# Turned softmax weights split one unit later, and head 10 turned on TensorE

## The chip, the cores and the metric

The kernel runs on one core of one Trainium2 chip. The metric is the device time of one execution in microseconds (us); several runs are made and their median is taken. Five engines have instruction queues of their own, each worked through in order: TensorE (PE, with its weight loads PEld), VectorE (DVE), ScalarE (ACT), GpSimd (POOL) and SyncE (SP), which here issues most of the DMA transfers.

## What is computed

One layer of an encoder on 256 tokens of width 2048: a normed input projection, windowed attention of 12 query heads on 4 key/value heads beside a small Fourier mixing group, an output projection, and a gated feed-forward network with a short convolution. The change touches the attention alone. Of the reference, that part is:

```python
scores = jnp.einsum('bnqkgd,bnskd->bnkgqs', qb, kb).astype(jnp.float32)
scores = scores * (HEAD_DIM ** -0.5)
scores = scores + alibi[None, None]
scores = jnp.where(valid[None, :, None, None], scores, NEG_INF)
m = jnp.maximum(jnp.max(scores, axis=-1, keepdims=True), sink_b)
p = jnp.exp(scores - m)
p = p / (jnp.sum(p, axis=-1, keepdims=True) + jnp.exp(sink_b - m))
out = jnp.einsum('bnkgqs,bnskd->bnqkgd', p.astype(v.dtype), vb)
```

Everything is float32. Products are made from two parts of each operand, a rounded high part ("hi") and the rest ("lo"), in three matmuls: hi by hi, lo by hi, hi by lo. So each tile that goes into a product is first split: ScalarE writes the high part, VectorE subtracts it from the original and writes the low part.

## The kernel before

The weights come in tiles of 1 MB, and each tile is one *unit*. `unit(i, work)` issues, in this order: the work hung up under `before[i]` (small matmuls of the attention), the unit's own matmuls, the work under `beside[i]` (vector and scalar work of the attention), the split of the weight tile of unit i+2 (`split`, L181 on ScalarE and L182 on VectorE) with the load of tile i+5, and the work under `behind[i]`. There is no scheduler: this order is the order in each engine's queue. Units 4 to 7 project v; units 8 to 23 project the heads in the order k0 q0 q1 q2 k1 q3 q4 q5 k2 q6 q7 q8 k3 q9 q10 q11; units 24 to 39 are the output projection (`moving_weights`, L333 to L335), which from unit 24 on reads the finished heads from the tiles `cat`; after that comes the feed-forward part.

A query head that is projected in unit s passes through the following steps, each hung up some units later:

- s+1, beside: `qk_out` adds the two halves of the projection (L631 ScalarE, L633 VectorE), and `qk_parts` splits the result into `qT` (L269 ScalarE, L270 VectorE). A key head does the same with one more multiply (L635) into `kT` (L643, L644).
- s+2, before: `scores` (L654, six matmuls of qT and kT). Beside: `scores_out` (L670 to L675, VectorE). Behind: `exps` (L684, L688, ScalarE).
- s+3, beside: `weigh` normalises the weights (L693 to L697, VectorE).
- The weights must then be turned (transposed). For the heads in `FLIPS` (0 to 10) VectorE turns 32x32 blocks (`flip_out`, L314, also at s+3), four DMAs write them to HBM (L317), and at s+4 `flip_in` reads them back in turned order (one DMA, L325) into the tile `flop`. At s+5, beside, `flip_parts` splits `flop` into `pt` (L739 ScalarE, L740 VectorE, two instructions each). Head 11 is turned on TensorE instead: `turn` at s+4, before (L704, four transposes), `turn_out` at s+4, beside, splits the result (L716, L717).
- `values`, before (L749, six matmuls of pt and v), at s+6 for the heads in `FLIPS` and at s+5 for the other; `values_out` in the same unit, beside: `feature_out` splits the scaled result into `cat` (L269, L270), squares it (`sq`, L489, ScalarE) and sums the squares on GpSimd (L490).

Within one unit's beside work the order before the change is: weigh and flip_out, flip_in, qk_out, values_out, turn_out, flip_parts, qk_parts, scores_out. On TensorE it is: values, turn, scores, then the unit's own matmuls.

Since the slots 8, 12, 16 and 20 are key heads, which have no scores and no values, the steps of a unit repeat with a period of four. Below, "unit 22 on VectorE" means the beside work and the split that are issued with unit 22, whenever VectorE comes to them.

Of the kernel before, what the change touches and what calls it, by code (L numbers as in the profile page):

```python
# [18 lines left out]
NH = 12  # L19
# [33 lines left out]
for _g in range(NKV):  # L53
    QK_ORDER += [("k", _g)] + [("q", _g * GQA + _i) for _i in range(GQA)]

FLIPS = range(NH - 1)
QK_FIRST = {n: (2, 2) if n in (8, 12) else (1, 0) for n in range(16)}
N_U, N_V, N_QK = 0, 4, 8
N_OUT = N_QK + len(QK_ORDER)
# [45 lines left out]
def block_kernel(  # L105
# [111 lines left out]
    def u_part(k, o, n, m=1):  # L217

        rows = ux[k // 4][:, (k < 4) * U_HEAD :].rearrange("p (k c) -> p k c", k=4)
        return rows[:, k % 4 : k % 4 + m, o : o + n]  # L220
# [152 lines left out]
    before, beside, behind = {}, {}, {}  # L373

    def at(when, i, f, *a):
        when.setdefault(i, []).append((f, a))
# [17 lines left out]
    for k in range(NK):  # L394
# [3 lines left out]
        n = 1 if c < 2 else 2  # L398
# [3 lines left out]
        if q % n == 0:  # L402
            w, h = u_part(k, 0, FW, n), hi[:, q : q + n, :]
# [225 lines left out]
    def qk_out(kind, h, ps):  # L629
        tmp = ph.tile([P, S], F32, tag="tmp", name=f"tmp_{kind}{h}", bufs=2)  # L630
        nc.scalar.activation(tmp, ps[:, S : 2 * S], AF.Copy)  # L631
        add = ph.tile([P, S], F32, tag="add", name=f"add_{kind}{h}", bufs=2)
        nc.vector.tensor_tensor(add, ps[:, 0:S], tmp, ALU.add)  # L633
        if kind == "k":
            nc.vector.tensor_tensor(add, add, r1b, ALU.mult)  # L635
        st["add", kind, h] = add
# [125 lines left out]
    for i in range(N_QK, N_OUT + 8):  # L762
        heads = {i - s: h for (kind, h), s in slot_of.items() if kind == "q"}
        new = [kh for kh, s in slot_of.items() if i - s == 1]
        for n, h in sorted(heads.items()):
            if n == 5 + (h in FLIPS):
                at(before, i, values, h)
        if 4 in heads and heads[4] not in FLIPS:
            at(before, i, turn, heads[4])
        if 2 in heads:  # L770
            at(before, i, scores, heads[2])
        if 3 in heads:
            at(beside, i, weigh, heads[3])
            if heads[3] in FLIPS:
                at(beside, i, flip_out, heads[3])
        if 4 in heads and heads[4] in FLIPS:
            at(beside, i, flip_in, heads[4])
        for kind, h in new:
            at(beside, i, lambda k=kind, h=h: qk_out(k, h, st.pop(("ps", k, h))))
        for n, h in sorted(heads.items()):  # L780
            if n == 5 + (h in FLIPS):
                at(beside, i, values_out, h)
        if 4 in heads and heads[4] not in FLIPS:
            at(beside, i, turn_out, heads[4])
        if 5 in heads and heads[5] in FLIPS:
            at(beside, i, flip_parts, heads[5])
        for kind, h in new:
            at(beside, i, qk_parts, kind, h)
        if 2 in heads:
            at(beside, i, scores_out, heads[2])  # L790
            at(behind, i, exps, heads[2])
# [59 lines left out]
    for n, (c, kq) in enumerate(OUT_ORDER):  # L851
        i = N_OUT + n
# [397 lines left out]
    i = up_index[n]  # L1250
# [158 lines left out]
```

## Time and profile before

| what | value |
|---|---|
| median of three runs | 945.75 us (945.72 to 945.88) |
| profiled execution, its own time | 945.7 us |
| profiled execution, first to last instruction (span) | 943.9 us |
| mean granted TensorE clock | 0.998 of full speed |
| TensorE busy | 930.4 us, 99% of the span |
| VectorE busy | 768.0 us, 81% |
| ScalarE busy | 541.6 us, 57% |
| GpSimd busy | 50.9 us, 5% |
| flip to HBM (L317) | 44 DMAs of 64 KB, 3.3 us to landing |
| HBM back to flop (L325) | 11 DMAs of 256 KB, 4.1 us to landing |

The profile is of one execution. A row of the timeline reads: start and duration in us, engine, line of the kernel, operation, output and inputs by their names in the program, shape, count, and in brackets how long the engine had been idle before and what it waited for. Rows of one engine can overlap a little, since the next instruction starts before the last has drained. Views that sum up waits give the total in us, the number of waits and the longest one.

### The profile page before, as it was taken

How to read it: one execution, taken by the hardware profiler on the slowest of the kernel's cores; microseconds unless marked ns; L12 is line 12 of the kernel's file. 1: busy time of each engine (PE TensorE's matmuls, PEld its weight loads, DVE VectorE, ACT ScalarE, POOL GpSimd, SP SyncE). 2: the span in 40 equal slices, each digit the busy share in tenths (PEclk: the TensorE clock that was granted, in tenths of full speed). 3: DMA queues.
4: the chain of work that ended last, by engine and by line, in shares of the span. 5: the costliest groups of instructions: out<-in, count | busy, mean ns of one | idle time of the engine just before them, and what ended most of it. 6: DMA issues, size and time to landing. Idle time of an engine off the chain costs nothing.

```text
span 943.9 us, 12848 instructions
## 1 busy us (share of the span) xinstructions
PE 930.4 (99%) x5025; PEld 804.7 (85%) x5025; DVE 768.0 (81%) x968; ACT 541.6 (57%) x673; POOL 50.9 (5%) x68
## 2 busy tenths in 40 slices
PE   9999999999999999999999999999999999999996
PEld 7888888888888888888888888888888888888885
DVE  7658888776677778799787997878989779989886
ACT  7755666654454555566555565555655556655553
POOL 0100000000000000000000000000000000000002
PEclk9999999999999999999999999999999999999999
DMA  9965666645556578877897779877788978779652
GB/s 365 308 224 167 212 213 193 220 178 205 196 214 211 182 230 254 260 257 234 257 262 254 243 235 277 250 263 228 262 242 238 299 246 261 230 231 274 208 178 89
DMA packets 48588, 220.63 MB, mean 234 GB/s; under 512 B 15856, under 2 KB 19184, under 8 KB 24976
## 3 DMA queue, kind: packets, MB, share of 16 engines
q1 hardware_dynamic: 43984, 190.32, 55.8%
q0 software_dynamic: 4544, 29.49, 16.8%
q8 instruction: 39, 0.64, 0.3%
q14 instruction: 21, 0.17, 0.0%
HBM read 214.81 MB, written 4.98 MB: 233 GB/s over the span
## 4 chain that ended last, share of the span: by engine, by line
PE 80%; DVE 7%; DMA 5%; ACT 4%; issue 2%; SPq 1%; POOL 0%; DVEq 0%; POOLq 0%; ACTq 0%
PE ps_val L350 25%; PE ps_gate L350 25%; PE ps_P L1118 3%; PE ps_P L1119 3%; PE ps_P L1120 3%; DVE lo L182 3%; PE ps_N L1118 3%; PE ps_N L1119 3%; PE ps_N L1120 3%; ACT hi L181 3%; PE ps_a L335 2%; PE ps_a L333 2%; PE ps_a L334 2%; DMA chan<-in_c_chan 2%; DMA ux<-in_w_u_x 1%
## 5 line engine op out<-in xcount | busy, mean ns | idle before, releaser
L182 DVE TENSOR_TENSOR lo<-raw,hi 128x2048 fp32r<-128x2048 f32 (+1 forms) x129 | 293.4, 2274 | 45.1 <-ACT hi L181 44.8
L181 ACT ACTIVATE hi<-raw 128x2048 fp32r<-128x2048 f32 (+1 forms) x129 | 245.2, 1902 | 35.6 <-PE ps_a L334 13.3
L350 PE MATMUL ps_val<-hU,hi 128*128 128x512 f32 x688 | 236.2, 389 | 0.0
L350 PE MATMUL ps_gate<-hU,hi 128*128 128x512 f32 x688 | 236.2, 389 | 0.0
L350 PE MATMUL ps_val<-hU,lo 128*128 128x256 f32 x688 | 189.9, 276 | 0.0
L350 PE MATMUL ps_gate<-hU,lo 128*128 128x256 f32 x688 | 189.9, 276 | 0.0
L350 PEld LDWEIGHTS ps_val<-hU,hi 128*128 128x128 f32 x688 | 129.1, 188 | 26.8
L350 PEld LDWEIGHTS ps_gate<-hU,hi 128*128 128x128 f32 x688 | 129.1, 188 | 26.8
L350 PEld LDWEIGHTS ps_gate<-hU,lo 128*128 128x128 f32 x688 | 129.1, 188 | 1.3
L350 PEld LDWEIGHTS ps_val<-hU,lo 128*128 128x128 f32 x688 | 129.1, 188 | 1.3
L893 ACT ACTIVATE ft_g<-ps_gate 128x256 f32<-128x256 f32 x43 | 16.5, 384 | 123.0 <-PE ps_gate L350 123.0
L893 ACT ACTIVATE ft_v<-ps_val 128x256 f32<-128x256 f32 x43 | 16.5, 384 | 91.8 <-PE ps_val L350 91.8
L350 PE MATMUL ps_q<-hT,hi 128*128 128x512 f32 x192 | 65.0, 391 | 0.0
L1118 PE MATMUL ps_P<-hi_P,op_P 128*128 128x512 f32 x144 | 56.0, 389 | 0.0
L1119 PE MATMUL ps_P<-hi_P,op_P 128*128 128x512 f32 x144 | 56.0, 389 | 0.0
L1120 PE MATMUL ps_P<-lo_P,op_P 128*128 128x512 f32 x144 | 56.0, 389 | 0.0
L350 PE MATMUL ps_q<-hT,lo 128*128 128x256 f32 x192 | 51.1, 277 | 0.0
L1010 DVE TENSOR_TENSOR lo_N<-sumw,hi_N 128x2048 fp32r<-128x2048 f32 (+1 forms) x20 | 41.5, 2076 | 9.4 <-ACT hi_N L1009 9.2
L1118 PE MATMUL ps_N<-hi_N,op_N 128*128 128x512 f32 x108 | 42.0, 389 | 0.0
L1119 PE MATMUL ps_N<-hi_N,op_N 128*128 128x512 f32 x108 | 42.0, 389 | 0.0
L1120 PE MATMUL ps_N<-lo_N,op_N 128*128 128x512 f32 x108 | 42.0, 389 | 0.0
L350 PEld LDWEIGHTS ps_q<-hT,hi 128*128 128x128 f32 x192 | 35.2, 188 | 6.6
(386 smaller groups left out, 1584.8 us busy)
## 6 DMA issues: line engine op xcount, KB each, us to landing
raw<-in_w_up SPq DMA_DIRECT2D x86, 1024.0 KB, 5.6
raw<-in_w_in SPq DMA_DIRECT2D x20, 1024.0 KB, 5.4
raw<-in_w_out SPq DMA_DIRECT2D x16, 1024.0 KB, 4.8
sumw<-in_w_down POOLq DMA_DIRECT2D x16, 1024.0 KB, 8.6
raw<-in_w_down_late SPq DMA_DIRECT2D x4, 1024.0 KB, 7.2
raw<-in_w_down_last SPq DMA_DIRECT2D x4, 768.0 KB, 4.2
turnp<-flip SPq DMA_DIRECT2D x44, 64.0 KB, 3.3
flop<-turnp SPq DMA_DIRECT2D x11, 256.0 KB, 4.1
```

The source lines that it names most:

```text
L181: nc.scalar.activation(hi[:, 0:n], raw[:, 0:n], AF.Copy)
L182: nc.vector.tensor_tensor(lo[:, 0:n], raw[:, 0:n], f32(hi[:, 0:n]), ALU.subtract)
L333: nc.tensor.matmul(ps, ah, wh, start=first and q == q0, stop=False)
L334: nc.tensor.matmul(ps, al, wh, start=False, stop=False)
L335: nc.tensor.matmul(ps, ah, wl, start=False, stop=last and q == q0 + len(kk) - 1)
L350: nc.tensor.matmul(ps[:, x], (hi, lo)[i][:, k * P : (k + 1) * P], hk(k)[:, x], start=n == 0 and k == 0, stop=n == len(order) - 1 and k == ...
L893: nc.scalar.activation(tmp, ps[:, S : 2 * S], AF.Copy)
L1010: nc.vector.tensor_tensor(lo, src, f32(hi), ALU.subtract)
L1118: nc.tensor.matmul(ps, o[:, 0, p, :], hi[:, s], start=first and p == 0, stop=False)
L1119: nc.tensor.matmul(ps, o[:, 1, p, :], hi[:, s], start=False, stop=False)
L1120: nc.tensor.matmul(ps, o[:, 0, p, :], lo[:, s], start=False, stop=last and p == n - 1)
```

## The change

`FLIPS` loses head 10, so heads 10 and 11 are now turned on TensorE. For the heads that stay in `FLIPS`, `flip_parts` moves from s+5 to s+6, and there from a place late in the beside work (after values_out) to its very beginning (ahead of weigh); `values` and `values_out` move from s+6 to s+7.

```diff
-FLIPS = range(NH - 1)
+FLIPS = range(NH - 2)
...
         for n, h in sorted(heads.items()):
-            if n == 5 + (h in FLIPS):
+            if n == 5 + 2 * (h in FLIPS):
                 at(before, i, values, h)
         if 4 in heads and heads[4] not in FLIPS:
             at(before, i, turn, heads[4])
         if 2 in heads:
             at(before, i, scores, heads[2])
+        if 6 in heads and heads[6] in FLIPS:
+            at(beside, i, flip_parts, heads[6])
         if 3 in heads:
             at(beside, i, weigh, heads[3])
...
         for n, h in sorted(heads.items()):
-            if n == 5 + (h in FLIPS):
+            if n == 5 + 2 * (h in FLIPS):
                 at(beside, i, values_out, h)
         if 4 in heads and heads[4] not in FLIPS:
             at(beside, i, turn_out, heads[4])
-        if 5 in heads and heads[5] in FLIPS:
-            at(beside, i, flip_parts, heads[5])
         for kind, h in new:
             at(beside, i, qk_parts, kind, h)
```

## The prediction

> **What bounds the kernel now.** I read the page first, then the waits between 92 and 190 us, then the timelines of TensorE, VectorE and ScalarE from 142 to 189 us.
>
> ```profile
> span 943.9 us, 12848 instructions
> PE 930.4 (99%) x5025; PEld 804.7 (85%) x5025; DVE 768.0 (81%) x968; ACT 541.6 (57%) x673; POOL 50.9 (5%) x68
> ```
>
> TensorE is busy all but 13.5 us of the span, so whatever delays its last wait delays the end. The waits show which idle time the change can touch:
>
> ```profile
> ACT sq L489 <- DVE cat L270: 23.8, 9, 3.0
> DVE lo L182 <- ACT hi L181: 7.3, 8, 1.3
> PEld ps_o L749 <- DVE pt L740: 5.5, 6, 1.7
> DVE pt L740 <- ACT pt L739: 5.0, 6, 0.9
> ```
>
> TensorE loses some 5.5 us because values waits for pt. The others say why pt is late: ScalarE's square of a head starts only after VectorE has written cat, ScalarE's pt is queued behind that square, and VectorE waits for ScalarE's pt. Two units on TensorE:
>
> ```profile
> 153.15 0.38 PE L749 MATMUL ps_o<-pt,v_hi 128*128 128x256 f32 x1 [1.44 <-DVE pt L740]
> ...
> 153.84 0.88 PE L654 MATMUL ps_s<-kT,qT 128*128 128x256 f32 x6
> 154.57 0.62 PE L350 MATMUL ps_q<-hT,hi 128*128 128x512 f32 x2
> ...
> 160.02 0.40 PE L749 MATMUL ps_o<-pt,v_hi 128*128 128x256 f32 x2
> ...
> 160.73 0.88 PE L654 MATMUL ps_s<-kT,qT 128*128 128x256 f32 x6
> 161.45 0.39 PE L333 MATMUL ps_a<-hi,cat 128*128 128x512 f32 x1
> ```
>
> A head's values takes 0.71 us (160.02 to 160.73), its scores 0.72, a unit's own matmuls 5.45 (154.57 to 160.02). The row at 153.15 is unit 23, waiting for the pt of unit 22 on VectorE. That engine's rows there, from the first instruction of unit 21 on:
>
> ```profile
> 142.96 0.15 DVE L693 TENSOR_TENSOR sm<-sm,ex 128x2 f32<-128x2 f32 x1
> ...
> 145.40 0.48 DVE L270 SCALAR_TENSOR_TENSOR cat<-ps_o,vec,cat 128x256 fp32r<-128x256 f32 x1
> 146.69 0.76 DVE L644 TENSOR_TENSOR kT<-add_k,kT 128x256 fp32r<-128x256 f32 x1 [0.82 <-ACT kT L643]
> ...
> 148.51 2.28 DVE L182 TENSOR_TENSOR lo<-raw,hi 128x2048 fp32r<-128x2048 f32 x1
> 150.71 0.15 DVE L693 TENSOR_TENSOR sm<-sm,ex 128x2 f32<-128x2 f32 x1
> ...
> 152.38 0.39 DVE L633 TENSOR_TENSOR add_q<-ps_q,tmp_q 128x256 f32<-128x256 f32 x1
> 152.69 0.74 DVE L740 TENSOR_TENSOR pt<-flop,pt 128x256 fp32r<-128x256 f32 x2
> 153.35 0.42 DVE L270 SCALAR_TENSOR_TENSOR qT<-add_q,qT 128x256 fp32r<-128x256 f32 x1
> 155.05 2.29 DVE L182 TENSOR_TENSOR lo<-raw,hi 128x2048 fp32r<-128x2048 f32 x1 [1.29 <-ACT hi L181]
> 157.26 0.42 DVE L633 TENSOR_TENSOR add_q<-ps_q,tmp_q 128x256 f32<-128x256 f32 x1
> ```
>
> Unit 21 lasts 7.75 us here (142.96 to 150.71), unit 22 6.55, and no row waits for TensorE: VectorE, paced by itself and ScalarE, runs a whole unit behind, and TensorE meets it. Decisive for the change: qT comes directly behind pt, ending at 153.77, and scores starts at 153.84. The wait for pt and a wait for qT bind at the same moment; taking the first away uncovers the second.
>
> **The change part by part.** I follow VectorE from unit 15, the first that differs, to the last scores, then TensorE to the output projection. Taken away: at s+5 the pt pair, 0.66 us on VectorE (152.69 to 153.35). Added: the same pair at the start of unit s+6, ahead of weigh. It waits for nothing there (flop landed a unit ago; ScalarE's pt follows exps and is done while VectorE still writes lo), but qT is still behind it, except in units 18 and 22, which lose the pair and receive a cat. What cat costs is shown by unit 21, where kT follows it as qT will, and by ScalarE's rows there:
>
> ```profile
> 145.97 0.39 ACT L489 ACTIVATE sq<-ps_o 128x256 f32<-128x256 f32 x1 [2.99 <-DVE cat L270]
> 146.25 0.41 ACT L643 ACTIVATE kT<-add_k 128x256 fp32r<-128x256 f32 x1
> 146.56 1.91 ACT L181 ACTIVATE hi<-raw 128x2048 fp32r<-128x2048 f32 x1
> ```
>
> From the start of cat: the square +0.57, ScalarE's kT (or qT) +0.85, VectorE's +1.29, hi from +1.16 to +3.07, so lo at +3.10 and the unit's end at +5.30 (2.20 for lo, 148.51 to 150.71). The four unit types become:
>
> - 17, 21 (key): 7.75 as now plus the pair 0.66: 8.41. The gap before kT was there before.
> - 18, 22: 1.67 to add (150.71 to 152.38), 0.31 for it, then 5.30 from cat: 7.28 against 6.55.
> - 15, 19, 23: the cat leaves. 0.66 for the pair, then from add as unit 22 does now (152.38 to 157.26): 5.54.
> - 16, 20, 24: the pair 0.66, 1.98 to cat, 5.31 after: 7.95; what pt leaves behind cat it takes at the start.
>
> Unit 15 starts at 100.25 in both, since unit 14 ends with lo waiting for ScalarE's hi:
>
> ```profile
> 98.04 2.29 DVE L182 TENSOR_TENSOR lo<-raw,hi 128x2048 fp32r<-128x2048 f32 x1 [1.22 <-ACT hi L181]
> 100.25 0.42 DVE L633 TENSOR_TENSOR add_q<-ps_q,tmp_q 128x256 f32<-128x256 f32 x1
> ```
>
> Then unit 22 starts at 100.25 + 5.54 + 7.95 + 8.41 + 7.28 + 5.54 + 7.95 + 8.41 = 151.33 instead of 150.71. Its qT starts at 151.33 + 1.98 + 1.29 = 154.60. How long it takes is not shown: GpSimd sums squares just then.
>
> ```profile
> 146.43 0.74 POOL L490 TENSOR_TENSOR sq_a<-sq_a,sq 128x256 f32<-128x256 f32 x1 [7.68 <-ACT sq L489]
> ...
> 931.62 1.30 POOL L1149 TENSOR_TENSOR xs<-xs,gfb 128x512 f32<-128x512 f32 x1 [0.84 <-ACT junkc L1137]
> ```
> ```profile
> 931.66 1.81 DVE L1175 SCALAR_TENSOR_TENSOR xs<-xs,rstd,gfb 128x512 f32<-128x512 f32 x1
> ...
> 938.23 1.41 DVE L1175 SCALAR_TENSOR_TENSOR xs<-xs,rstd,gfb 128x512 f32<-128x512 f32 x2
> ```
>
> The kT at 146.69 took 0.76 beside such a sum, and an instruction of qT's kind 1.81 instead of some 0.7 at the end of the kernel. Bounds: 0.42 as at 153.35, 0.76 as kT. I take 0.76, the same place in the unit. So qT ends at 155.36 and scores of unit 23 starts at 155.43 (0.07 on, as before): 1.59 later than 153.84.
>
> TensorE from there: scores and own matmuls 0.73 + 5.45, to 161.61; unit 24 values 0.71, scores 0.72 and 5.47 (half of 169.13 to 180.07 below), to 168.51; unit 25 values, to 169.22. Its scores, the last that meet VectorE, need qT of unit 24: start 151.33 + 7.28 + 5.54 = 164.15, qT's end +0.66 + 1.98 + 1.29 + 0.76, and 0.07, is 168.91: no wait. They start at 169.22 instead of 168.42:
>
> ```profile
> 168.42 0.88 PE L654 MATMUL ps_s<-kT,qT 128*128 128x256 f32 x6
> 169.13 0.40 PE L333 MATMUL ps_a<-hi,cat 128*128 128x512 f32 x1
> ...
> 180.07 0.40 PE L749 MATMUL ps_o<-pt,v_hi 128*128 128x256 f32 x2
> ...
> 180.78 0.60 PE L704 MATMUL ps_t<-ident,sc 128*128 128x128 f32 x4
> 181.14 0.48 PE L333 MATMUL ps_a<-hi,cat 128*128 128x512 f32 x1
> ...
> 186.72 0.40 PE L749 MATMUL ps_o<-pt,v_hi 128*128 128x256 f32 x2
> ```
>
> That is +0.80. **Behind the last meeting there is more TensorE work than before.** Unit 26 had neither values nor turn; now it has head 8's values (0.71), which was done ahead of the last wait, and head 10's turn (0.36, 180.78 to 181.14), after which the unit's matmuls take 5.58 instead of 5.47: 1.18 together. Units 27 and 28 keep their counts, heads 9 and 10 changing places.
>
> Costed at nothing: head 10's flip (0.6 of VectorE) and five SP DMAs fall away in units where TensorE no longer waits. flop keeps its buffer a unit longer, but whoever claims that one comes after the split in the same queue; without that cover the price would be a late return of one flop. The split of head 10's turned weights in unit 26 ends, by the same offsets, near 182.0, TensorE asks for it near 182.1: I allow up to 0.3. cat of head 7 is written near 174.3 and read near 178. The weight tiles' lo parts stay over 3 us ahead from unit 24 on.
>
> Sum: 0.80 + 1.18 = +1.98 on the profiled execution's own 945.7 (span 943.9 and 1.8 around it, 0.05 from the median 945.75): **947.7 us**. With qT at 0.42, 0.35 less: 947.3. If the moved pair costs VectorE nothing because its units have gaps anyway, unit 22 starts 0.62 earlier: 947.1 at most. Upwards, 0.3 for the turn and 0.1 (my allowance) for each of the seven unit lengths added: 948.7.
>
> [...] TensorE will stand longer in one piece than before: it reaches unit 19 near 122.8 and gets scores at 126.2; it reaches unit 23 near 152.3 and waits to 155.4.
>
> [...]
>
> **The rivals.**
>
> 1. *The clock drops after a long wait.* For it: waits of 3.4 and 3.1 us where the longest was 1.7. Against: the mean granted clock stayed at 0.998 with waits of 1.7. A drop at unit 19 is hidden in the wait at unit 23; one at unit 23 is not. If matmuls run at half speed for as long as the wait lasted, 1.5 us are lost: 949.2; over a whole unit, 5.45: 953.
>
> 2. *TensorE is freed* (faster). With a whole unit between pt and values, the 5.5 us of waits vanish and only the turn's 0.36 + 0.11 is added: 945.7 - 5.5 + 0.5 = 940.7. For it: VectorE waits 7.3 and 5.0 us for ScalarE, and those gaps might close. It decides when unit 22's qT ends before 152.3, 3 us earlier than the sum. Against: ScalarE's order puts the square in front of qT as it did in front of pt, so the gaps move and do not close. A part of it, 2 us sooner, would already be faster by more than 0.2%.
>
> 3. *It does not do what it says, near nothing lost:* the wait goes from pt to qT at its old time, and only the turn is added: 945.7 + 0.5 = 946.2.
>
> **How the numbers follow.** The forecast, with its variants, gets 0.82, rival 1 0.06, rival 2 0.06, rival 3 0.06. About 0.2% (1.9 us, a bound at 947.6) is what a measurement can tell from no change. The forecast lies on that bound: I give it 0.48 above and 0.34 within. So faster 0.06, within 0.2% 0.40, slower 0.54. The forecast's own range is 946.9 to 948.7; the range given, 946.3 to 949.2, takes in rival 3 partly and the lower case of rival 1, and leaves out rival 2.
>
> **What would show it.** In the profile after: no wait of values for pt; instead weight loads of scores waiting for VectorE's qT, some 3 us each in units 19 and 23 and little elsewhere; VectorE's units 17 and 21 near 8.4 us and 18 and 22 near 7.3; 0.8 us gaps before qT with ScalarE's qT as the cause; qT at 0.76 beside GpSimd's sum; the first out-projection matmul after the last scores near 169.9 and units 26 to 28 without waits; granted clock 1.00. Wrong if TensorE reaches unit 23's scores before 154, or if it waits after 170.

## The result, and the profile after

| | before | after |
|---|---|---|
| median of eleven runs each, side by side | 946.07 us | 947.55 us (947.29 to 949.38) |
| ratio, after to before | | 1.0019, 95% interval 1.0011 to 1.0027 |
| profiled execution, its own time | 945.7 us | 948.0 us |
| span | 943.9 us | 946.2 us |
| mean granted TensorE clock | 0.998 | 0.996 |

The kernel is slower by 1.0 to 2.6 us. Whether that is over 0.2% the interval leaves open; that it is slower, it does not.

The first lines of the page after, to be held against the two shown of before:

```profile
span 946.2 us, 12845 instructions
PE 932.9 (99%) x5029; PEld 807.5 (85%) x5029; DVE 767.3 (81%) x966; ACT 540.8 (57%) x672; POOL 50.8 (5%) x68
```

TensorE's four instructions more and the three fewer of VectorE and ScalarE are head 10's way of being turned. TensorE's busy time grew by 2.5 us and the span by 2.3; head 10's four transposes are one row of 0.60 us (at 182.94), so matmuls that were there before took longer. The waits between 92 and 192 us (total, number, longest):

```profile
ACT sq L489 <- DVE cat L270: 23.3, 9, 3.3
...
DVE lo L182 <- ACT hi L181: 7.5, 11, 1.3
DVE qT L270 <- ACT qT L269: 6.0, 9, 0.9
PEld ps_s L654 <- ACT qT L269: 4.1, 3, 2.8
PE ps_s L654 <- ACT qT L269: 3.4, 2, 2.6
...
PEld ps_s L654 <- DVE qT L270: 1.1, 3, 0.5
...
PE ps_s L654 <- DVE qT L270: 0.6, 2, 0.3
```

The same window before had, besides the 5.5 us of weight loads that the prediction shows, a row of the matmuls themselves: `PE ps_o L749 <- DVE pt L740: 4.3, 6, 1.5`.

No values waits for pt any more: the 5.5 us are gone. In their place scores waits for qT, and nearly as long: 5.2 us by the weight loads (4.1 and 1.1), 4.0 us by the matmuls (3.4 and 0.6). VectorE's 5.0 us for ScalarE's pt have become 6.0 us for ScalarE's qT. The gap before lo stays as well. VectorE's rows from unit 21 to the start of unit 24, as far as the prediction dated them:

```profile
143.19 0.76 DVE L740 TENSOR_TENSOR pt<-flop,pt 128x256 fp32r<-128x256 f32 x2
...
151.63 0.15 DVE L693 TENSOR_TENSOR sm<-sm,ex 128x2 f32<-128x2 f32 x1
...
153.62 0.46 DVE L270 SCALAR_TENSOR_TENSOR cat<-ps_o,vec,cat 128x256 fp32r<-128x256 f32 x1
154.90 0.75 DVE L270 SCALAR_TENSOR_TENSOR qT<-add_q,qT 128x256 fp32r<-128x256 f32 x1 [0.81 <-ACT qT L269]
156.70 2.29 DVE L182 TENSOR_TENSOR lo<-raw,hi 128x2048 fp32r<-128x2048 f32 x1 [1.05 <-ACT hi L181]
158.90 0.76 DVE L740 TENSOR_TENSOR pt<-flop,pt 128x256 fp32r<-128x256 f32 x2
...
164.49 0.75 DVE L740 TENSOR_TENSOR pt<-flop,pt 128x256 fp32r<-128x256 f32 x2
```

Unit 21 lasts 8.44 us (143.19 to 151.63), unit 22 7.27 (to 158.90), unit 23 5.59 (to 164.49): forecast were 8.41, 7.28 and 5.54. In unit 22 qT comes 1.28 behind cat and takes 0.75. TensorE where it meets VectorE, and at the last scores:

```profile
125.61 0.50 PE L654 MATMUL ps_s<-kT,qT 128*128 128x256 f32 x2 [2.56 <-ACT qT L269]
126.40 1.22 PE L654 MATMUL ps_s<-kT,qT 128*128 128x256 f32 x4 [0.28 <-DVE qT L270]
127.42 1.05 PE L350 MATMUL ps_q<-hT,hi 128*128 128x512 f32 x2
...
133.93 0.40 PE L749 MATMUL ps_o<-pt,v_hi 128*128 128x256 f32 x2
...
154.91 0.50 PE L654 MATMUL ps_s<-kT,qT 128*128 128x256 f32 x2 [0.85 <-ACT qT L269]
155.70 0.74 PE L654 MATMUL ps_s<-kT,qT 128*128 128x256 f32 x4 [0.28 <-DVE qT L270]
156.28 0.62 PE L350 MATMUL ps_q<-hT,hi 128*128 128x512 f32 x2
...
169.35 0.88 PE L654 MATMUL ps_s<-kT,qT 128*128 128x256 f32 x6
170.07 0.40 PE L333 MATMUL ps_a<-hi,cat 128*128 128x512 f32 x1
...
182.23 0.40 PE L749 MATMUL ps_o<-pt,v_hi 128*128 128x256 f32 x2
```

The out-projection of unit 25 starts at 170.07 instead of 169.13, which is 0.94 later. Values of head 8 and the turn then stand in unit 26, and unit 27 begins at 182.23, where before it began at 180.07: 2.16 later, without a wait in between. That is the 2.3 us of the span, nearly whole. Some 0.18 of it is no doing of the change: VectorE's lo of unit 12, ahead of everything that differs, starts at 84.64 us in this execution and at 84.46 in the one before.

One thing in these rows was forecast otherwise. Unit 19's own matmuls run from 127.42 to 133.93, 6.51 us instead of 5.45. The windows view, around that place (columns: busy time and count of each of the five engine rows, then granted clock, DMA share, GB/s):

```profile
122.80:126.20 3.40, 0.76 (x5) 0.35 (x3) 2.55 (x6) 1.33 (x3) 0.73 (x1) 1.00 0.85 255
126.20:129.70 3.50, 3.30 (x11) 2.91 (x12) 2.45 (x3) 2.05 (x4) 0.00 (x0) 0.51 0.80 201
```

Directly behind the wait of 2.56 us TensorE was granted half its clock for some 3.4 us. Unit 23, with a wait of 0.85 and one of 0.28, kept the full clock.

### The profile page after: what moved, and what is told of

It is laid out like the page before. It is cut to its first block, busy times and chain, and to the rows that moved or that the text cites. A ratio compares the mean times of both kernels' runs of the same rounds, so it can differ in the third digit from the quotient of the medians.

```text
span 946.2 us, 12845 instructions
## 1 busy us (share of the span) xinstructions
PE 932.9 (99%) x5029; PEld 807.5 (85%) x5029; DVE 767.3 (81%) x966; ACT 540.8 (57%) x672; POOL 50.8 (5%) x68
## 4 chain that ended last, share of the span: by engine, by line
PE 85%; DVE 6%; ACT 5%; issue 2%; DMA 1%; DVEq 0%; SPq 0%; POOLq 0%; POOL 0%; ACTq 0%
PE ps_val L350 25%; PE ps_gate L350 25%; PE ps_P L1120 3%; PE ps_P L1118 3%; PE ps_P L1119 3%; PE ps_N L1120 2%; PE ps_N L1118 2%; PE ps_N L1119 2%; ACT hi L181 2%; PE ps_a L335 2%; PE ps_a L333 2%; PE ps_a L334 2%; DVE lo L182 2%; PE ps_ff L333 1%; PE ps_ff L335 1%
```

## The experiments

Three questions were open. Are the two late terms, the turn and the moved split, what the sum says they are? Does qT wait because ScalarE's square stands ahead of it? And what does the half clock cost? Each kernel but one was timed against the kernel before; times are medians, ratios have their 95% intervals, and the experiments' own tables of waits are from 92 to 192 us. The traces are of single executions, which stand apart before any edit takes effect: VectorE's lo of unit 12 starts at 84.64 us in the changed kernel, 84.19 in e2, 84.31 in e6, 84.74 in e7 and 84.57 in e9. Such a head start is named below where it matters.

### The turn alone (e1_turn_only)

The kernel before, with one line of the change:

```diff
-FLIPS = range(NH - 1)
+FLIPS = range(NH - 2)
```

> The kernel before, with head 10 alone turned on TensorE; split and values stay at s+5 and s+6. Theory A (the time is set where scores meets VectorE's qT, and TensorE work behind that meeting is added in full): the turn comes in unit 26, behind the last meeting, so only 0.36 + 0.11 us is added: ratio to before 1.0005. Rival B (the turned head is what costs, by its split on VectorE and a wait of its values): most of the 1.5 to 2 us of the change, ratio 1.0015 or more, with a wait of values in unit 27.

Measured: 946.28 us, ratio 1.0004 (0.9995 to 1.0012). TensorE's rows:

```profile
168.74 0.88 PE L654 MATMUL ps_s<-kT,qT 128*128 128x256 f32 x6
...
180.88 0.40 PE L749 MATMUL ps_o<-pt,v_hi 128*128 128x256 f32 x2
```

From the last scores to the next values it is 12.14 us, where before it was 11.65 (168.42 to 180.07): 0.49, forecast at 0.36 + 0.11. The waits of values for pt were still there (5.1 us over 5). So the turn is the small part of the loss.

### The split early again, the products late (e2_split_early)

The changed kernel, with flip_parts back at s+5, behind values_out; values stays at s+7:

```diff
-        if 6 in heads and heads[6] in FLIPS:
-            at(beside, i, flip_parts, heads[6])
...
+        if 5 in heads and heads[5] in FLIPS:
+            at(beside, i, flip_parts, heads[5])
```

> The changed kernel with the split of the turned weights back in its old place (s+5, behind values_out), values still at s+7, head 10 on TensorE. Theory A: VectorE's unit types last 7.94, 7.75, 7.88 and 4.87 us, qT of unit 22 ends near 153.9, scores of unit 23 starts near 154.0, those of unit 25 near 167.8 without a wait, and then 1.18 us more TensorE work: +0.6 us, ratio 1.0006. Rival B (where the split stands makes no difference, the unit's delay of values is the cost): as the changed kernel, ratio 1.0016 to 1.0020.

Measured: 946.88 us, ratio 1.0009 (1.0000 to 1.0018). The interval holds theory A's 1.0006 and the lower part of rival B's range, so the time decides nothing between them. The trace says more. VectorE and then TensorE:

```profile
152.16 0.47 DVE L270 SCALAR_TENSOR_TENSOR cat<-ps_o,vec,cat 128x256 fp32r<-128x256 f32 x1
153.44 1.10 DVE L740 TENSOR_TENSOR pt<-flop,pt 128x256 fp32r<-128x256 f32 x2 [0.82 <-ACT pt L739]
154.46 0.41 DVE L270 SCALAR_TENSOR_TENSOR qT<-add_q,qT 128x256 fp32r<-128x256 f32 x1
```
```profile
125.45 2.06 PE L654 MATMUL ps_s<-kT,qT 128*128 128x256 f32 x6 [2.73 <-ACT qT L269]
134.96 0.40 PE L749 MATMUL ps_o<-pt,v_hi 128*128 128x256 f32 x2
...
154.93 0.88 PE L654 MATMUL ps_s<-kT,qT 128*128 128x256 f32 x6
```

What stands next behind the square now is pt, so the gap of 0.82 moves to pt, and so does GpSimd's sum: the pair takes 1.10 instead of 0.74. qT then takes 0.41 and ends at 154.87, 0.78 earlier than in the changed kernel, but 0.45 of that is the head start. Theory A had it near 153.9. Most of what is missing went in unit 15: ScalarE's early pt, which starts at 100.88, had waited 2.87 us there for flop to land, and the unit lasted 5.98 us on VectorE (99.98 to 105.96) where theory A has 4.87. The changed kernel, which splits a unit later, has no such wait. And the half clock came here for two stretches: from the scores at 125.45 to the next values 9.51 us pass instead of the 6.17 of full speed (0.72 and 5.45), so that TensorE came to unit 23 only at 154.93, and there found qT ready. With the clock up it would have come sooner, but not far: the low part of qT was there only at 154.87.

### The square out of the way, before and after (e3, e4, e7, e8)

If ScalarE's square delays pt before and qT after, then taking it out of the way must help both kernels. In all four the square and GpSimd's sum are issued by a function of their own:

```diff
     def values_out(h):
-        feature_out(st.pop(("o", h))[:, 0:S], h, vcol(V_GA + h), sq_a, h == 0)
+        ps = st["o", h][:, 0:S]
+        cat[h] = cat_pool.tile([P, 512], F32R, tag="cat", name=f"cat{h}")
+        split_scaled(cat[h], ps, vcol(V_GA + h))
...
+        for n, h in sorted(heads.items()):
+            if n == 5 + 2 * (h in FLIPS):
+                at(behind, i, values_square, h)
```

With `behind` it stands behind the weight split and the exponentials (e3 for the changed kernel, e4 for the one before, there with `5 + 1 *`); with `beside`, appended last there, it stands behind qT and ahead of hi (e7 changed, e8 before).

> The changed kernel with ScalarE's square of each attention head (and so GpSimd's sum) issued behind the split and the exps of the unit instead of right after cat. Theory A: qT no longer stands behind the square; VectorE's unit types shrink to 7.2, 7.66, 6.54 and 5.54, TensorE waits under 1 us in units 19 and 23, and the time falls to 942.6, or to 945 if GpSimd's sums now hold up VectorE's split of pt: ratio to before 0.9967 to 0.9992. Rival C (the half clock after the long wait is the cost): at most the 1.1 us that unit 19 lost is regained: ratio 1.0007 or more.

> The kernel before with the same move of the squares. Theory A: the wait of VectorE's pt and qT for ScalarE goes, VectorE's units shrink to 6.65, 7.0, 6.55 and 5.0, and TensorE's 5.5 us of waits for pt nearly vanish: 940.5, up to 943 if GpSimd's sums hold up VectorE elsewhere: ratio 0.9945 to 0.997, and lower than with the change, which adds 1.18 us of TensorE work behind the last wait or less. Rival D (pt is late because VectorE is full, not because of the square): ratio 0.999 to 1.000, the waits for pt stay over 4 us.

> The changed kernel with ScalarE's square moved behind qT (ahead of the weight tile's hi), so that qT is not behind the square and GpSimd's sum falls on scores_out, which reads PSUM. Theory A: qT starts 0.1 us after cat ends and takes 0.42; VectorE's units last 7.6, 8.1, 7.0 and 5.5; scores of unit 23 starts near 152.7; 945.0 against the 947.6 of the change, ratio to before 0.998 to 0.9995 (less gain if the clock halves after unit 19 or 23). Rival (the square's place does not matter): ratio 1.0016 or more.

> The kernel before with the square moved behind qT in the same way. Theory A: pt and qT no longer wait for the square, and GpSimd's sum falls where VectorE reads PSUM: VectorE's units last near 7.0, 7.4, 6.6 and 5.3, TensorE's waits for pt drop from 5.5 to about 2 us, limited now by the transfers of the turned weights: ratio 0.995 to 0.9975, near the kernel with the square behind everything (0.9961). Rival D (VectorE is simply full): ratio 0.999 to 1.000.

| | the kernel before with it | the changed kernel with it |
|---|---|---|
| square last, behind | e4: 942.25 us, 0.9961 (0.9948 to 0.9973) | e3: 945.69 us, 0.9999 (0.9990 to 1.0008) |
| square behind qT | e8: 942.57 us, 0.9963 (0.9950 to 0.9975) | e7: 946.35 us, 1.0004 (0.9995 to 1.0013) |

In the kernel before it came as expected, twice, and both are faster than the two kernels that the change compares. The waits of e4 that answer to those of before:

```profile
ACT pt L739 <- DMA flop<-turnp: 12.4, 7, 2.5
...
PEld ps_o L749 <- DVE pt L740: 2.1, 2, 1.4
...
DVE pt L740 <- ACT pt L739: 1.2, 4, 0.6
```

values' waits fell from 5.5 to 2.1 us (1.9 in e8), VectorE's for ScalarE's pt from 5.0 to 1.2. ScalarE's pt now waits for flop to land; it is early. So the square was what made pt late, together with GpSimd's sum, which moved with it; what the sum does alone is measured in the changed kernel only (e5).

In the changed kernel the mechanism is seen too, but the time fell short of both expectations: e3 ends 0.0007 above its range, e7 0.0009 above the one that it had for a clock kept up. In e7 the gap before qT is closed (VectorE), yet look at TensorE:

```profile
152.41 0.47 DVE L270 SCALAR_TENSOR_TENSOR cat<-ps_o,vec,cat 128x256 fp32r<-128x256 f32 x1
152.97 0.43 DVE L270 SCALAR_TENSOR_TENSOR qT<-add_q,qT 128x256 fp32r<-128x256 f32 x1
```
```profile
152.99 1.54 PE L654 MATMUL ps_s<-kT,qT 128*128 128x256 f32 x6 [1.95 <-ACT qT L269]
154.33 1.05 PE L350 MATMUL ps_q<-hT,hi 128*128 128x512 f32 x2
...
161.08 0.40 PE L749 MATMUL ps_o<-pt,v_hi 128*128 128x256 f32 x2
```
```profile
153.60:157.10 3.50, 3.50 (x13) 3.04 (x14) 1.91 (x1) 2.44 (x4) 0.57 (x1) 0.51 0.96 259
```

qT follows cat by 0.56 instead of 1.28 us, and scores begins at 152.99, 1.92 earlier than in the changed kernel. But TensorE waits 1.95 us for it, and the half clock comes in unit 23, where no later wait hides it: scores 1.34 and own matmuls 6.75 us instead of 0.72 and 5.45. Of the 1.92 us 0.65 arrive at the last scores (168.70 against 169.35). In e3 it is the same (a wait of 2.10, then 6.60 us for the own matmuls, at a clock of 0.50 from 152.8 to 156.2), and there GpSimd's sums fall on other instructions:

```profile
149.46 0.70 DVE L693 TENSOR_TENSOR sm<-sm,ex 128x2 f32<-128x2 f32 x1
...
156.56 1.30 DVE L740 TENSOR_TENSOR pt<-flop,pt 128x256 fp32r<-128x256 f32 x2
```
```profile
148.92 1.22 POOL L769 TENSOR_TENSOR sq_a<-sq_a,sq 128x256 f32<-128x256 f32 x1 [7.03 <-ACT sq L768]
154.66 2.58 POOL L769 TENSOR_TENSOR sq_a<-sq_a,sq 128x256 f32<-128x256 f32 x1 [4.52 <-ACT sq L768]
```

The sum at 148.92 starts while VectorE writes lo, takes 1.22 instead of 0.73, and sm behind it takes 0.70 instead of 0.15; the one at 154.66 takes 2.58, through lo and into the pt pair, which takes 1.30 instead of 0.76. Some 0.55 us each time. For pt the expectation of e3 had allowed (945 us), for sm it had not.

### GpSimd's sum taken away (e5_no_sums)

The changed kernel without the sums of squares of heads 1 to 11:

```diff
-            nc.gpsimd.tensor_tensor(sq, sq, one, ALU.add)
+            if slot >= NH:
+                nc.gpsimd.tensor_tensor(sq, sq, one, ALU.add)
```

> The changed kernel without GpSimd's sums of the squares of heads 1 to 11 (the norm of the attention group then sees head 0 alone); ScalarE's squares stay. Theory A: qT and kT behind cat fall from 0.75 to 0.42 us, the unit lengths of VectorE stay (lo waits for ScalarE's hi, 3.10 us after cat, either way), and the scores of units 19 and 23 start some 0.3 us earlier. Rival E (the 0.75 is not GpSimd's doing): qT stays at 0.75.

One execution was taken, 950.18 us; its time is not used, since VectorE was 1.8 us late as early as 61 us, ahead of any edit, and TensorE waited at unit 15 already. The row it was made for holds all the same (VectorE):

```profile
155.20 0.47 DVE L270 SCALAR_TENSOR_TENSOR cat<-ps_o,vec,cat 128x256 fp32r<-128x256 f32 x1
156.42 0.43 DVE L270 SCALAR_TENSOR_TENSOR qT<-add_q,qT 128x256 fp32r<-128x256 f32 x1 [0.75 <-ACT qT L269]
158.22 2.29 DVE L182 TENSOR_TENSOR lo<-raw,hi 128x2048 fp32r<-128x2048 f32 x1 [1.37 <-ACT hi L181]
```

Without the sum qT takes 0.43, with it 0.75; the gap in front of it stays, 0.75 against 0.81. So the length of qT is GpSimd's doing and the gap is not. The changed kernel itself agrees: the square of head 0 has no sum, and the qT behind that head's cat, at 109.89 us, takes 0.43 after a gap of 0.76. lo comes 3.08 behind cat with the sum (153.62 to 156.70) and 3.02 without it: ScalarE's hi sets it, so the sum costs the unit nothing and only its qT 0.3.

It is not qT alone: the pt pair took 1.10 us beside a sum (e2, at 153.44) and 0.76 without one (e2, at 158.47). But not every instruction of VectorE grows: scores_out (L670) took 0.42 us beside a sum (e7, at 166.89) and 0.42 without one (e7, at 159.66).

### The clock kept up (e6_keep_busy, e9_after_square_after_qt_busy)

Both add matmuls of kT with itself ahead of scores, into the tile that scores then overwrites. e6 is the changed kernel with 18 of them for heads 6 and 9 (units 19 and 23), e9 is e7 with 12 for head 9:

```diff
         qT, kT = qk_sb.pop(("q", h)), qk_sb["k", h // GQA]
+        for _ in range(18 if h in (6, 9) else 0):
+            nc.tensor.matmul(ps[:, 0:S], kT[:, 0:P], kT[:, 0:S], start=True, stop=True)
```

> The changed kernel with 18 extra matmuls ahead of the scores of heads 6 and 9 (units 19 and 23), some 2.1 us each, into the bank that scores then overwrites: TensorE works through its long waits. Theory A: the half clock after unit 19 goes (granted clock in that stretch back to 1.00), TensorE arrives at unit 23 a microsecond earlier and waits that much longer: time unchanged, ratio to before 1.0015 to 1.0022. Rival C (the half clock costs time in the end): 1.1 us less, ratio 1.0004 to 1.0008.

> The changed kernel with the square behind qT, as measured before at 1.0004, and besides 12 matmuls of kT with itself ahead of the scores of head 9 (unit 23); their result is overwritten. A, the clock: without them TensorE waited 1.95 us there, and then ran its scores in 1.34 instead of 0.72 and the unit's own matmuls in 6.75 instead of 5.45 us. The 12 take some 1.4 us of that wait, the granted clock stays at 1.00, unit 23's own matmuls take 5.45, and the last scores that meet VectorE come 1.9 us earlier, near 166.8 instead of 168.70 (VectorE's qT for them ends at 166.6, so no new wait). Ratio 0.9980 to 0.9990. B, the slow matmuls come from something else (operands that arrive late, the weight tile, memory contention): they stay slow, the 12 change nothing or add, and the ratio stays at 1.0004 or goes up.

Measured: e6 947.70 us, ratio 1.0016 (1.0007 to 1.0025), like the changed kernel's 1.0019. Its TensorE:

```profile
126.65 0.62 PE L350 MATMUL ps_q<-hT,hi 128*128 128x512 f32 x2
...
132.25 0.39 PE L751 MATMUL ps_o<-pt,v_hi 128*128 128x256 f32 x2
...
152.22 2.31 PE L653 MATMUL ps_s<-kT 128*128 128x256 f32 x18
154.57 0.50 PE L656 MATMUL ps_s<-kT,qT 128*128 128x256 f32 x2
```

Unit 19's own matmuls take 5.60 us, and TensorE comes to unit 23 at 152.22 instead of some 153.9, which is 1.4 us sooner beyond e6's head start of 0.33. It gains nothing by that, since qT is no earlier: scores begins at 154.57 instead of 154.91, and that 0.34 is the head start. What the half clock takes at unit 19 is paid out of the wait at unit 23.

e9 945.20 us, ratio 0.9996 (0.9987 to 1.0005), the mechanism as theory A had it, the time outside its range. Its TensorE:

```profile
150.67 1.60 PE L653 MATMUL ps_s<-kT 128*128 128x256 f32 x12
152.80 1.20 PE L656 MATMUL ps_s<-kT,qT 128*128 128x256 f32 x6 [0.53 <-ACT qT L269]
153.84 0.63 PE L350 MATMUL ps_q<-hT,hi 128*128 128x512 f32 x2
...
159.31 0.40 PE L751 MATMUL ps_o<-pt,v_hi 128*128 128x256 f32 x2
```

The same wait, filled: the granted clock is 1.00 from 150 to 168 us, where e7 had 0.51 from 153.60 to 157.10, and unit 23's own matmuls take 5.47 instead of 6.75; the next values comes 1.77 earlier (159.31 against 161.08, 0.17 of it head start), and so does all behind it (the last scores at 166.93, forecast near 166.8). That rules out late operands and memory as the cause of the slow matmuls: the clock it is. Against e7 the ratio moved by 0.0008, 0.8 us, half of what the two traces show, and the two intervals overlap. The likely reason is that not every execution of e7 loses its clock. The record has the mean granted clock of each: four executions of e7, with 0.998 or 0.999, took 945.16 to 945.90 us, and seven, with 0.995 to 0.997, 946.22 to 948.14. In e3 six with 0.997 to 0.999 took 944.75 to 945.69 and five with 0.995 to 0.997 946.33 to 947.83. The figure is coarse (e9's traced execution has 0.997 without a stretch), but it fits medians that mix executions which lost the clock with others that kept it. In the changed kernel itself the three executions with the lowest clock, 0.994, took 947.39 to 947.63 and are not the longest, which agrees with e6: there the loss is hidden.

## Why the prediction was right

**The mechanism.** It held as put: taking away the wait for pt uncovered the wait for qT, since qT stood directly behind pt (the waits above), and what holds qT back is the order on ScalarE (e4 and e8 for pt, e7 for qT).

**VectorE's units.** 8.41, 7.28, 5.54 and 7.95 were forecast; the trace has 8.44, 7.27, 5.59 and, for units 16, 20 and 24, 7.89, 8.00 and 7.95. Added up, unit 22 starts at 151.63 instead of 151.33: 0.17 was there already at unit 15 (it is the offset of the two executions), 0.13 came over seven units, where 0.1 for each had been allowed.

**qT.** It comes 1.28 behind cat and takes 0.75; forecast 1.29 and 0.76. Choosing the upper bound, by the place in the unit, was right, and e5 shows the cause.

**The meeting.** Scores of unit 23 was to end its wait at 155.43. Its first two matmuls began at 154.91, since they need only the high part that ScalarE writes, and the rest at 155.70. The prediction had tied all six to VectorE's low part. It ended at 156.28, against 156.16 by the sum: two small errors of opposite sign, 0.30 later and 0.18 earlier.

**The last scores and what stands behind them.** +0.80 was forecast, +0.93 measured (169.35 against 168.42), without a wait as forecast. Unit 26 was to bring 1.18 and brought 1.22 (2.16 less 0.94). The 0.3 allowed for the turn's split was not needed. In all 1.98 were forecast and 2.16 are in the trace at unit 27, some 0.18 of it the offset of the executions; the medians differ by 1.48 and the ratio says 1.0 to 2.6. That the forecast of 947.7 lies only 0.15 from the median 947.55 is partly luck: the kernel before ran at 946.07 in the eleven runs, 0.37 above the 945.7 that the sum starts from, and the difference came out 0.5 lower.

**The clock.** Here one of the prediction's own signs was wrong: "granted clock 1.00". Rival 1's first half came true, a drop at unit 19 (0.51 from 126.20 to 129.70), and was hidden in unit 23's wait, as the rival said it would be; e6 shows no cost of it (1.0016 against 1.0019). Its second half, a drop at unit 23, stayed away. After the first one TensorE came some 1.4 us later to unit 23 (153.9 against 152.22 in e6, less the head start) and waited only 0.85 and 0.28 there, where the prediction had some 3; that the shorter wait is what spared it is likely by e7 and e3, and was not tried by itself. Why the drop at unit 19 was not in the sum: the waits of up to 1.7 us that left the clock alone were taken as evidence against it, though they were shorter than what was to come. A half clock the trace of before does have, but only behind TensorE's last matmul, which ends at 935.85 us: 0.50 from 940.0 to the end of the span. The rival's 1.5 and 5.45 us were the author's estimates of what a drop costs; the one at unit 19 lasted some 3.4 us and made the unit's own matmuls 1.06 us longer (6.51 against 5.45).

**TensorE freed (rival 2).** The prediction and this rival count 5.5 us as lost by TensorE; that is the weight loads' row, and the matmuls themselves waited 4.3. The gap before qT moved and did not close, as was said against it. Freed at qT's side in e7, it is given back to the clock.

## What to carry to other kernels

Before a wait is taken away, look at what the waiting engine asks for next, and whether the same queue makes it in the next instruction; then the wait changes its name and hardly its length (4.3 us of the matmuls before, 4.0 after). Look one engine further for what both are queued behind: here a square for a norm, needed by nobody for many units, and moving that in the kernel before gave 0.4% where moving the late part itself lost 0.2%. And work that is moved from before an engine's last wait to behind it is paid in full: 0.71 of the 2.16 us here are the six matmuls of head 8's values, which before stood ahead of the last scores.

## What the runs showed of the hardware

The clock fell behind shorter waits than the 3.1 and 3.4 us that the prediction's rival 1 rested on. Between 90 and 200 us each half-clock stretch seen followed a wait of TensorE of 1.95 to 2.73 us (1.95 in e7, 2.10 in e3, 2.56 after, 2.73 in e2), and in e5 the six matmuls of scores behind a wait of 1.79 us took 1.48 us, as they did in e3 at half clock. None followed the waits of up to 1.5 us (1.46 before, 1.47 in e1, 1.22 in e4 and e9, all at a clock of 1.00; 1.22 in e7, where the unit's own 128x512 matmuls took 0.39 us behind the wait as ahead of it). What waits between 1.5 and 1.79 us do, no run here shows. The stretches were of some 3.4 us (0.51 over 3.5 us after and in e7, 0.50 over 3.4 us in e3; 0.51 over 6.9 us in e2). A unit's own matmuls, 5.45 us at full clock, took 6.51 after, 6.60 in e3 and 6.75 in e7; the scores that fell into a stretch took 1.34 in e7 and 1.48 in e3, and 1.04 in e9, which kept its clock.

GpSimd's addition of 128x256 took 0.74 us while VectorE waited (e7, at 153.43) and 0.73 beside qT (after, at 154.63). Where it overlapped VectorE's 2.29 us lo, it took 1.22 and 2.58 in e3 and 1.23 in e4 (at 146.41), and the VectorE instruction behind lo then lost about 0.55 us (sm 0.70 instead of 0.15 in e3 and e4, the pt pair 1.30 instead of 0.76 in e3). So moving an operation of an engine that is busy 5% of the span was not free here.
